# Full 128-row matmuls in the attention of a two-layer streaming encoder

## The chip, the core and the metric

The kernel runs as one program on one core of a Trainium2 chip. The metric is the device time of one execution in microseconds. Every kernel is run several times, and the median is given. The trace of one execution was taken by the hardware profiler.

## What is computed

One inference step of a hybrid encoder trunk with two layers, for 512 new frames of one stream (the prompt) and 32 frames of a running stream (the sample, with 128 cached positions). Per layer:

```python
h = rmsnorm(x)
cq, ckv, kr, hq, hf, hi, hg, ga, gb = split(h @ w_in)        # one input projection
q = rmsnorm(cq) @ w_uq          # 8 heads, 128 plain + 64 rotary columns each
k_nope, v = rmsnorm(ckv) @ w_ukv ; k_pe = rope(kr)           # k_pe is shared by the heads
o_a = softmax((q_nope k_nope^T + rope(q_pe) k_pe^T) / sqrt(192)) v   # block-causal for the prompt
o_b = gated linear recurrence (4 heads)                      # causal, chunk by chunk
x = x + (sigmoid(ga) * (o_a @ w_a) + sigmoid(gb) * (o_b @ w_b)) @ w_out
x = x + conv_ffn(rmsnorm(x))                                 # 1024 -> 2 x 2816 -> 1024
```

All inputs and outputs are float32. The sample's 32 queries see all 160 of their own keys (128 cached, 32 new), without a mask.

## The kernel before, in words

Activations lie with features on the 128 partitions and 544 tokens (512 + 32) along the free dimension. Each float32 operand of a product is split into a high and a low part of a reduced float32 type (`split`, lines 152 to 154: ScalarE makes the high part, VectorE subtracts it), and a product is three matmuls: high by high, low by high, high by low. The large products are made by `linear` (line 185); its matmuls have line 198.

Smaller work (the recurrence of a head, the attention of a head) is written as generators that a queue called `side` steps through between the matmuls of the large products, at a pace that is set by hand: ten steps of one head's attention are spread over the products that stand beside it (lines 860 to 871). The program is laid down in that order, a planner at compile time then fixes each engine's stream, and it may move an instruction within its engine's stream. Each engine runs its stream in order and waits on semaphores of the others.

The attention of a head is `attend` (line 725). `rope_q` leaves the rotary queries of a head as four stacked groups of 32 rows: high, high, low, low. The rotary keys' high part `krh` holds the 64 key rows twice, on 128 rows, so that one matmul with `krh` (line 737) gives high and low query by high key. Their low part `krl` is kept on 64 rows only, and is multiplied with the first 64 rows of the queries (line 738). A block of scores (`scores`, line 734) is thus five matmuls into one PSUM bank, the last of them over 64 rows. There are four prompt blocks of 128 queries in a head (256, 256, 384 and 512 keys wide), tile `sc`, and one sample block of 160 keys, tile `ss`.

A prompt block goes on to `softmax` (line 717: maximum, scaled negation, exponential with sum on ScalarE, reciprocal, multiplication), to `turn` (transposes of 128 x 128, line 764), and to `weigh` (line 778). The sample block is computed for 128 queries, of which the last 32 rows are copied out of PSUM by ScalarE (line 793) and go through softmax as a tile `sP` of 32 rows. `sample_turn` transposes it in two pieces (lines 799 and 800: 32 rows by 128 and 32 rows by 32), splits each piece, and `sample_weigh` multiplies by the values in six matmuls (line 812): three over 128 rows, three over 32 rows.

PSUM tiles of the small work come from a ring of four banks (`s_ps`). Weights are cast by ScalarE; the subtraction for some of them runs on GpSimd (`pool=True`, line 176).

Of the kernel before, what the change touches and what calls it, by code (L numbers as in the profile page):

```python
# [18 lines left out]
P = 128  # L19
L = 2  # L20
# [31 lines left out]
class Late:  # L52
    """A value whose instructions come with its first use, or within the product before."""

# [9 lines left out]
class Pieces:  # L64
    """Weights of n row blocks, of which each group of eight is fetched at its first use."""

# [12 lines left out]
class Side:  # L79
    """Work whose instructions are laid between those of the large products."""  # L80

# [7 lines left out]
    def pace(self, rate):  # L89
        """Steps to take for each tick of the large products."""  # L90
        self.rate, self.owed = rate, 0.0
# [23 lines left out]
def trunk(ctx, tc, io):  # L115
# [123 lines left out]
    class Norm:  # L239
        """Sum of squares over feature blocks, as they come."""  # L240

# [15 lines left out]
    def prep(x, gcol, norm, name, vector=False):  # L257
        """Split of gain * x, and its share of the norm's sum."""
        if norm is not None:
            norm.add(x, vector)  # L260
        hi, lo = bt(f"hhi_{name}"), bt(f"hlo_{name}")
        g = vec[:, gcol:gcol + 1]
        nc.scalar.activation(hi, x, AF.Copy, scale=g)
        nc.vector.scalar_tensor_tensor(lo, x, g, hi, op0=ALU.mult, op1=ALU.subtract)
        return hi, lo
# [29 lines left out]

    # Lower bounds of the forget gates: softmax over the layers, cumulated.
    lbs, omls = [], []
# [33 lines left out]
    for l in range(L):  # L331
# [21 lines left out]
        if l == 0:  # L353
            # The first products run while the norm is still on its way.
            early[U_HF] = product(U_HF, "hf0_", first)
            early[U_HQ] = product(U_HQ, "hq0_")
            ws = load_w(io["w_in"][l, U_HI], ND, P, "hi0_0")
            r.get()
            early[U_HI] = linear(ws, h, TH, "ps_hi0_0", apart=True)
# [5 lines left out]
        with ExitStack() as mixer:  # L365
# [3 lines left out]
            krh = mp.tile([P, KW], F32R, name=f"krh{l}")  # L369
            krl = mp.tile([64, KW], F32R, name=f"krl{l}")  # L370
            gates = dram.tile([2 * ND, P, T], F32, name=f"gates{l}")
            ob = []

            with ExitStack() as hs:
# [17 lines left out]
                def levels(q0, Q, K, F1, FL, A, ntok, top, name):  # L392
                    """Decayed products q k within chunks of 128 rows, by halves of ever larger
                    blocks: every factor is a product of forget gates, at most one."""
                    nch = ntok // P
# [36 lines left out]
                def scan(hh, q0, Q, K, f, vt):  # L432
                    """Outputs and final state of a head over the prompt."""
                    nm = f"{l}_{hh}"
# [38 lines left out]
                def scan_sample():  # L473
                    """The four heads' sample rows as one block of 128."""
                    flat = lambda x: x.rearrange("p h t -> p (h t)")
# [79 lines left out]

                # Compressed queries, latents, rotary keys, merge gates.
                def gate(i):
# [32 lines left out]
                def rotary_keys(z):  # L590
                    zsw = tt(f"zks{l}")
                    for q in range(4):
                        src, dst = z[(q ^ 1) * 32:(q ^ 1) * 32 + 32, :], zsw[q * 32:q * 32 + 32, :]
                        nc.scalar.activation(dst, src, AF.Copy, scale=-1.0 if q % 2 == 0 else 1.0)
                    kr = h1.tile([P, KW], F32, name=f"kr{l}")
                    nc.sync.dma_start(kr[0:64, SP:SP + PAST], io["c_kr"][l])
                    nc.sync.dma_start(kr[64:128, SP:SP + PAST], io["c_kr"][l])
                    nc.vector.tensor_mul(z, z, cos)
                    nc.vector.tensor_mul(zsw, zsw, sin)
                    nc.vector.tensor_add(kr[:, 0:SP], z[:, 0:SP], zsw[:, 0:SP])  # L600
                    nc.vector.tensor_add(kr[:, SP + PAST:KW], z[:, SP:T], zsw[:, SP:T])
                    nc.sync.dma_start(io["krope"][l, :, 0:SP], kr[0:64, 0:SP])
                    nc.sync.dma_start(io["krope"][l, :, SP:T], kr[0:64, SP + PAST:KW])
                    nc.scalar.copy(krh, kr)
                    nc.vector.tensor_sub(krl, kr[0:64, :], krh[0:64, :])

# [23 lines left out]
            def merge(j):  # L630
                """A block of both branches' gated sum."""
                sg, mb = tt(f"sga{l}_{j}"), tt(f"mb{l}_{j}")
# [10 lines left out]

            # Attention.
            oa = []
            with ExitStack() as asx:
# [10 lines left out]
                def rope_q(hq):  # L657
                    """Rotated queries of four heads, as rows (high, high, low, low)."""
                    raw = fetch_w(io["w_qr"][l, hq], 2 * QR_K * P, f"qr{l}_{hq}")
# [25 lines left out]
                def project(hd):  # L685
                    """Queries, keys and (for two heads) values of a head."""
                    nm = f"{l}_{hd}"
# [37 lines left out]
                def attend(hd):  # L725
# [8 lines left out]
                    def scores(ps, qs, ks):  # L734
                        for i, (a, b) in enumerate(rows):
                            nc.tensor.matmul(ps, a[:, qs], b[:, ks], start=(i == 0), stop=False)  # L736
                        nc.tensor.matmul(ps, q4[:, qs], krh[:, ks], start=False, stop=False)
                        nc.tensor.matmul(ps, q4[0:64, qs], krl[:, ks], start=False, stop=True)

# [11 lines left out]
                    def turn(half, pr, kps):  # L751
                        """Probabilities with the keys on partitions, split."""
                        nkb = 2 * half + 2
# [31 lines left out]

                    # The sample's rows are the last 32 of the last 128 queries.
                    NK = PAST + SS

                    def sample_scores():
                        ps = s_ps(f"ss{nm}")  # L790
                        scores(ps[:, :NK], slice(T - P, T), slice(SP, KW))
                        sP = ap.tile([SS, NK], F32, tag="sP", name=f"sP{nm}")
                        nc.scalar.copy(sP, ps[P - SS:P, :NK])
                        softmax(sP, sP, SS, f"{nm}_s")
                        return sP

                    def sample_turn(sP):
                        ps = s_ps(f"spt{nm}")
                        nc.tensor.transpose(ps[:, 0:SS], sP[:, 0:PAST], ident[0:SS, 0:SS])
                        nc.tensor.transpose(ps[0:SS, SS:2 * SS], sP[:, PAST:NK], ident[0:SS, 0:SS])  # L800
                        sph = ap.tile([P, 2 * SS], F32R, tag="sph", name=f"sph{nm}")
                        spl = ap.tile([P, 2 * SS], F32R, tag="spl", name=f"spl{nm}")
                        split(sph[:, 0:SS], spl[:, 0:SS], ps[:, 0:SS])
                        split(sph[0:SS, SS:2 * SS], spl[0:SS, SS:2 * SS], ps[0:SS, SS:2 * SS])
                        return sph, spl

                    def sample_weigh(sph, spl):
                        ps = s_ps(f"spo{nm}")
                        i = 0
                        for a, rr in ((0, P), (1, SS)):  # L810
                            for v, p in ((vh, sph), (vl, sph), (vh, spl)):
                                nc.tensor.matmul(
                                    ps[:, 0:SS], v[0:rr, 4 + a, vo:vo + P], p[0:rr, a * SS:(a + 1) * SS],
                                    start=(i == 0), stop=(i == 5),
# [28 lines left out]
                def gated_b(j):  # L843
                    """The gated share of branch b."""
                    if not ob:
# [42 lines left out]

        # Gated feed-forward network.
        with ExitStack() as fs:  # L890
# [13 lines left out]
            def final(t, ps, x):  # L904
                """Half of the tokens' output, when their last block is there."""
                hs = slice(t * TH, (t + 1) * TH)
# [9 lines left out]
                for j in range(0, ND, 2):  # L916
                    # The first half's share stays in place, the second's goes out in pairs of blocks.
                    pair = bt(f"yo{j}", F32) if t else None
# [44 lines left out]
            def down(j):  # L963
                """The weights of an output block; the last has its own place for most of them."""
                return Pieces(lambda k: load_w(
# [42 lines left out]
def _units(w, cols):  # L1008
    """Columns of [L, K, N] weights as [L, unit, 128 rows, K/128 x unit width]."""
    l, k, _ = w.shape  # L1010
# [5 lines left out]
def _rows(v):  # L1016
    """[..., n * 128] vectors as [128, ... x n]."""
    return np.ascontiguousarray(np.asarray(v).reshape(-1, P).T)
# [81 lines left out]
```

## Time and profile before

| | |
|---|---|
| median of 3 runs | 1913.16 us |
| lowest and highest | 1912.61 and 1913.16 us |
| span of the profiled execution, first to last instruction | 1910.8 us |
| between that span and the median of the runs | 2.4 us |
| TensorE busy | 1887.2 us (99% of the span) |
| VectorE, ScalarE, GpSimd busy | 1092.7, 797.1, 312.2 us |

The profiled execution has no time of its own beside its span; the runs' median stands in for it, and the 2.4 us are what lies before the first and after the last instruction. Busy TensorE is not TensorE at its peak: its instructions overlap and their ends are modelled, so what one costs is read from the distance between the starts of one and the next. The attention of the first layer lies at about 271 to 467 us of the span, that of the second at about 1213 to 1409 us.

### The profile page before, as it was taken

How to read it: one execution, taken by the hardware profiler on the slowest of the kernel's cores; microseconds unless marked ns; L12 is line 12 of the kernel's file. 1: busy time of each engine (PE TensorE's matmuls, PEld its weight loads, DVE VectorE, ACT ScalarE, POOL GpSimd, SP SyncE). 2: the span in 40 equal slices, each digit the busy share in tenths (PEclk: the TensorE clock that was granted, in tenths of full speed). 3: DMA queues.
4: the chain of work that ended last, by engine and by line, in shares of the span. 5: the costliest groups of instructions: out<-in, count | busy, mean ns of one | idle time of the engine just before them, and what ended most of it. 6: DMA issues, size and time to landing. Idle time of an engine off the chain costs nothing.

```text
span 1910.8 us, 36056 instructions
## 1 busy us (share of the span) xinstructions
PE 1887.2 (99%) x14680; PEld 1847.6 (97%) x14680; DVE 1092.7 (57%) x2113; ACT 797.1 (42%) x1454; POOL 312.2 (16%) x474
## 2 busy tenths in 40 slices
PE   7999999999999999999999999999999999999997
PEld 7999999899999999999999999998999999999997
DVE  7765865666465555533375667656655655555224
ACT  4222866554344333332232248564533433333231
POOL 3011021221212222100011110212112122222001
PEclk9999999999999999999999999999999999999999
DMA  5121432333542222234322124323235422222332
GB/s 181 57 70 67 131 122 83 95 102 104 194 158 89 89 89 89 89 95 125 102 91 70 57 80 143 119 80 107 93 126 190 138 85 87 87 88 87 103 96 75
DMA packets 75526, 197.29 MB, mean 103 GB/s; under 512 B 10208, under 2 KB 14304, under 8 KB 75360
## 3 DMA queue, kind: packets, MB, share of 16 engines
q1 hardware_dynamic: 75360, 194.98, 30.9%
q8 instruction: 116, 1.90, 0.4%
q14 instruction: 50, 0.41, 0.1%
HBM read 165.68 MB, written 24.81 MB: 100 GB/s over the span
## 4 chain that ended last, share of the span: by engine, by line
PE 97%; DVE 1%; DMA 1%; issue 0%; SPq 0%; ACT 0%; DVEq 0%; ACTq 0%
PE ps_uv L198 14%; PE ps_ua L198 14%; PE ps_d L198 13%; PE ps_gate L198 10%; PE ps_pa L198 5%; PE ps_o L198 5%; PE A L401 3%; PE ps_q L198 3%; PE ps_pb L198 3%; PE ps_hg L198 3%; PE ps_hq L198 2%; PE ps_hi L198 2%; PE ps_hf L198 2%; PE ps_cq L198 2%; PE sc L736 2%; PE ps_v L710 2%
## 5 line engine op out<-in xcount | busy, mean ns | idle before, releaser
L176 DVE TENSOR_TENSOR wlo_d<-raw_d,whi_d 128x512 fp32r<-128x512 f32 x96 | 62.5, 655 | 149.5 <-ACT whi_d L175 149.5
L198 PE MATMUL ps_uv<-hlo_f,whi_uv 128*128 128x272 f32 x704 | 145.9, 289 | 0.0
L198 PE MATMUL ps_ua<-hlo_f,whi_ua 128*128 128x272 f32 x704 | 145.9, 289 | 0.0
L198 PE MATMUL ps_ua<-hhi_f,wlo_ua 128*128 128x272 f32 x704 | 145.8, 288 | 0.0
L198 PE MATMUL ps_ua<-hhi_f,whi_ua 128*128 128x272 f32 x704 | 145.6, 288 | 0.0
L198 PE MATMUL ps_uv<-hhi_f,whi_uv 128*128 128x272 f32 x704 | 145.6, 288 | 0.0
L198 PE MATMUL ps_uv<-hhi_f,wlo_uv 128*128 128x272 f32 x704 | 145.4, 288 | 0.0
L198 PE MATMUL ps_d<-il,whi_d 128*128 128x272 f32 x660 | 136.9, 289 | 0.0
L198 PE MATMUL ps_d<-ih,wlo_d 128*128 128x272 f32 x660 | 136.6, 288 | 0.0
L198 PE MATMUL ps_d<-ih,whi_d 128*128 128x272 f32 x660 | 136.2, 288 | 0.0
L175 ACT CAST whi_d<-raw_d 128x512 fp32r<-128x512 f32 x96 | 55.8, 585 | 175.5 <-PE ps_d L198 143.7
L175 ACT CAST whi_ua<-raw_ua 128x512 fp32r<-128x512 f32 x88 | 54.7, 621 | 165.3 <-PE ps_ua L198 157.9
L175 ACT CAST whi_uv<-raw_uv 128x512 fp32r<-128x512 f32 x96 | 59.6, 621 | 142.5 <-PE ps_uv L198 134.1
L198 PEld LDWEIGHTS ps_ua<-hhi_f,wlo_ua 128*128 128x128 f32 x704 | 110.8, 188 | 0.2
L198 PEld LDWEIGHTS ps_ua<-hhi_f,whi_ua 128*128 128x128 f32 x704 | 110.9, 188 | 0.0
L198 PEld LDWEIGHTS ps_uv<-hhi_f,whi_uv 128*128 128x128 f32 x704 | 110.9, 188 | 0.0
L198 PEld LDWEIGHTS ps_uv<-hhi_f,wlo_uv 128*128 128x128 f32 x704 | 110.7, 188 | 0.0
L198 PEld LDWEIGHTS ps_ua<-hlo_f,whi_ua 128*128 128x128 f32 x704 | 110.4, 188 | 0.0
L198 PEld LDWEIGHTS ps_uv<-hlo_f,whi_uv 128*128 128x128 f32 x704 | 110.4, 188 | 0.0
L198 PEld LDWEIGHTS ps_d<-ih,whi_d 128*128 128x128 f32 x660 | 103.6, 188 | 0.0
L198 PEld LDWEIGHTS ps_d<-il,whi_d 128*128 128x128 f32 x660 | 103.6, 188 | 0.0
L198 PEld LDWEIGHTS ps_d<-ih,wlo_d 128*128 128x128 f32 x660 | 103.2, 188 | 0.0
(469 smaller groups left out, 5274.8 us busy)
## 6 DMA issues: line engine op xcount, KB each, us to landing
raw_ua<-in_w_up SPq DMA_DIRECT2D x44, 512.0 KB, 3.2
raw_uv<-in_w_up SPq DMA_DIRECT2D x44, 512.0 KB, 3.2
raw_gate<-in_w_in SPq DMA_DIRECT2D x32, 512.0 KB, 3.7
raw_d<-in_w_dn SPq DMA_DIRECT2D x32, 512.0 KB, 3.5
gates<-z_gate SPq DMA_DIRECT2D x32, 272.0 KB, 2.9
raw_pa<-in_w_pa SPq DMA_DIRECT2D x16, 512.0 KB, 3.5
raw_wo<-in_w_o SPq DMA_DIRECT2D x16, 512.0 KB, 3.7
raw_d<-in_w_dn SPq DMA_DIRECT2D x16, 384.0 KB, 3.1
```

Of the source, the lines that this page charges most:

```text
L175: nc.scalar.copy(hi[:, :n], part)
L176: (nc.gpsimd if pool else nc.vector).tensor_sub(lo[:, :n], part, hi[:, :n])
L198: nc.tensor.matmul(ps[t][:, 0:n], w, x[:, t * n:(t + 1) * n], start=(i == 0), stop=(i == last),)
L401: nc.tensor.matmul(ps[:, s], kk[:, s], qq[:, s], start=True, stop=True)
L710: nc.tensor.matmul(ps[:, :2 * P], lat[k][x][:, s], wv[k][w], start=(i == 0), stop=(i == 5))
L736: nc.tensor.matmul(ps, a[:, qs], b[:, ks], start=(i == 0), stop=False)
```

## The change

The low part of the rotary keys is kept on all 128 rows, so that the matmul of line 738 runs over 128 rows. (Its two further groups of rows add low query by low key, a term that was left out before.) The sample's softmax runs on all 128 query rows, straight out of PSUM, into a tile of the ring that the prompt blocks use (`tag="p"`, four buffers); the columns 160 to 255 of that tile are zeroed by GpSimd. The transposes become two of 128 x 128, the split takes the last 32 columns of both in one ScalarE and one VectorE instruction, and the sample's six weighting matmuls all run over 128 rows (the padded rows are zero). The diff also removes comments and docstrings; its core:

```diff
-            krl = mp.tile([64, KW], F32R, name=f"krl{l}")
+            krl = mp.tile([P, KW], F32R, name=f"krl{l}")
...
-                    nc.vector.tensor_sub(krl, kr[0:64, :], krh[0:64, :])
+                    nc.vector.tensor_sub(krl, kr, krh)
...
-                        nc.tensor.matmul(ps, q4[0:64, qs], krl[:, ks], start=False, stop=True)
+                        nc.tensor.matmul(ps, q4[:, qs], krl[:, ks], start=False, stop=True)
...
-                        sP = ap.tile([SS, NK], F32, tag="sP", name=f"sP{nm}")
-                        nc.scalar.copy(sP, ps[P - SS:P, :NK])
-                        softmax(sP, sP, SS, f"{nm}_s")
+                        sP = ap.tile([P, 512], F32, tag="p", name=f"sP{nm}", bufs=4)
+                        nc.gpsimd.memset(sP[:, NK:2 * P], 0.0)
+                        softmax(sP[:, :NK], ps[:, :NK], P, f"{nm}_s")
                         return sP
 
                     def sample_turn(sP):
                         ps = s_ps(f"spt{nm}")
-                        nc.tensor.transpose(ps[:, 0:SS], sP[:, 0:PAST], ident[0:SS, 0:SS])
-                        nc.tensor.transpose(ps[0:SS, SS:2 * SS], sP[:, PAST:NK], ident[0:SS, 0:SS])
-                        sph = ap.tile([P, 2 * SS], F32R, tag="sph", name=f"sph{nm}")
-                        spl = ap.tile([P, 2 * SS], F32R, tag="spl", name=f"spl{nm}")
-                        split(sph[:, 0:SS], spl[:, 0:SS], ps[:, 0:SS])
-                        split(sph[0:SS, SS:2 * SS], spl[0:SS, SS:2 * SS], ps[0:SS, SS:2 * SS])
+                        pw = ps[:, 0:2 * P].rearrange("p (a q) -> p a q", a=2)
+                        for a in range(2):
+                            nc.tensor.transpose(pw[:, a, :], sP[:, a * P:(a + 1) * P], ident)
+                        sph = ap.tile([P, 2, SS], F32R, tag="sph", name=f"sph{nm}")
+                        spl = ap.tile([P, 2, SS], F32R, tag="spl", name=f"spl{nm}")
+                        split(sph, spl, pw[:, :, P - SS:P])
                         return sph, spl
...
-                        for a, rr in ((0, P), (1, SS)):
+                        for a in range(2):
                             for v, p in ((vh, sph), (vl, sph), (vh, spl)):
                                 nc.tensor.matmul(
-                                    ps[:, 0:SS], v[0:rr, 4 + a, vo:vo + P], p[0:rr, a * SS:(a + 1) * SS],
+                                    ps[:, 0:SS], v[:, 4 + a, vo:vo + P], p[:, a, :],
```

## Rows read from the trace of the kernel before

**Rows 1.** The cores: span and mean granted TensorE clock.

```profile
core 0: 1910.8 us, clock 0.997
```

**Rows 2.** The chain that ended last: shares of the span by engine.

```profile
PE 97%; DVE 1%; DMA 1%; issue 0%; SPq 0%; ACT 0%; DVEq 0%; ACTq 0%
```

**Rows 3.** First layer's attention, engines' busy us (instructions) in the columns' order.

```profile
core 0: us, PE busy (x) PEld busy (x) DVE busy (x) ACT busy (x) POOL busy (x), PEclk, DMA share, GB/s
271.20:466.70 195.50, 194.59 (x1372) 177.17 (x1370) 123.39 (x356) 102.90 (x269) 31.66 (x32) 1.00 0.31 98
```

**Rows 4.** Line 738's matmuls: ns min/median/max, first and last start, shapes.

```profile
L738 PE MATMUL sc<-krl,qr x64: 379/408/498, 294.0 to 1398.4; 64*128 64x256 f32 x32, 64*128 64x384 f32 x16, 64*128 64x512 f32 x16
...
L738 PE MATMUL ss<-krl,qr x16: 337/338/342, 303.8 to 1400.2; 64*128 64x160 f32 x16
```

**Rows 5.** Timeline of PE, first and second score block of a head: start, length.

```profile
342.65 0.28 PE L737 MATMUL sc<-krh,qr 128*128 128x256 f32 x1
342.86 0.38 PE L738 MATMUL sc<-krl,qr 64*128 64x256 f32 x1
343.17 0.39 PE L736 MATMUL sc<-kh,qh 128*128 128x256 f32 x1
343.40 0.28 PE L736 MATMUL sc<-kh,ql 128*128 128x256 f32 x1
343.52 0.28 PE L736 MATMUL sc<-kl,qh 128*128 128x256 f32 x1
```

**Rows 6.** Timeline of PEld, weight loads around the third score block's end.

```profile
345.62 0.19 PEld L737 LDWEIGHTS sc<-krh,qr 128*128 128x128 f32 x1
346.06 0.18 PEld L738 LDWEIGHTS sc<-krl,qr 64*128 64x128 f32 x1 [0.25 <-issue]
```

**Rows 7.** Timeline of PE around a sample score block's end.

```profile
372.77 0.28 PE L737 MATMUL ss<-krh,qr 128*128 128x160 f32 x1
...
373.61 0.41 PE L198 MATMUL ps_q<-cqh,whi_qk 128*128 128x272 f32 x2
373.86 0.42 PE L198 MATMUL ps_q<-cqh,wlo_qk 128*128 128x272 f32 x2
```

**Rows 8.** Timeline of PE: three full transposes, then the sample's two.

```profile
335.74 0.49 PE L764 MATMUL pt<-ident,p 128*128 128x128 f32 x3
335.99 0.50 PE L198 MATMUL ps_gate<-hlo_in,whi_gate 128*128 128x272 f32 x2
336.32 0.41 PE L198 MATMUL ps_gate<-hhi_in,whi_gate 128*128 128x272 f32 x2
...
337.08 0.41 PE L198 MATMUL ps_gate<-hhi_in,whi_gate 128*128 128x272 f32 x2
...
337.98 0.41 PE L198 MATMUL ps_gate<-hlo_in,whi_gate 128*128 128x272 f32 x2
```

**Rows 9.** Timeline of PE, the sample's weighting of the same head.

```profile
340.45 0.26 PE L812 MATMUL spo<-sph,vl 128*128 128x32 f32 x1
340.56 0.26 PE L812 MATMUL spo<-spl,vh 128*128 128x32 f32 x1
...
341.19 0.52 PE L198 MATMUL ps_pb<-obh,whi_pb 128*128 128x272 f32 x2
341.54 0.29 PE L198 MATMUL ps_pb<-obh,wlo_pb 128*128 128x272 f32 x1
```

**Rows 10.** Timeline of DVE, softmax of the first blocks; idle before, releaser.

```profile
346.58 0.11 DVE L744 MEMSET sc<- 64x64 f32 x1 [1.51 <-PE sc L738]
...
347.46 0.53 DVE L723 TENSOR_SCALAR p<-p,st 128x128 f32<-128x128 f32 x2
```

**Rows 11.** Timeline of PE, the first transpose that reads those probabilities.

```profile
348.04 0.27 PE L764 MATMUL pt<-ident,p 128*128 128x128 f32 x1
```

**Rows 12.** POOL's waits in the first layer's attention: us, times, longest.

```profile
POOL wlo_qk L176 <- ACT whi_qk L175: 57.7, 15, 14.9
```

**Rows 13.** POOL's costliest groups: busy us, mean ns of one, idle before.

```profile
L582 POOL MEMSET lr<- 128x96 f32 x4 | 0.7, 178 | 45.0 <-DVE latl L154 45.0
```

## Prediction

> **What bounds the kernel now.** I read the cores first: one core, 1910.8 us from first to last instruction, clock 0.997, so TensorE runs at its upper level of 2.4 GHz nearly throughout and the clock has nothing to give [rows 1]. Then the chain that ended last: 97% of it is TensorE [rows 2]. A change that takes time out of TensorE's stream therefore shortens the whole, as far as nothing else comes to stand in its place. Third, the table by stretch for the attention of the first layer, the stage that the change touches: TensorE is busy 194.6 of 195.5 us there, VectorE 123.4, ScalarE 102.9, GpSimd 31.7 [rows 3]. Only a shorter TensorE stream can help in this stage, and the other three have room. The second layer's attention is the same program on other weights, and the score matmuls start in both, from 294 to 1398 us [rows 4].
>
> "Busy" hides how well TensorE is used, so the fourth view is the timeline, where I compare starts. In a run of full matmuls 256 columns wide the next one starts 0.12 us after the last (343.40 to 343.52). Around the 64-row matmul it is otherwise: it starts 0.21 us after the full one ahead of it, the next full one 0.31 us after it, and the one behind that another 0.23 us later [rows 5]. The weight loads tell why. The load for the full matmul at line 737 starts ahead of its matmul, while another one streams; the 64-row load starts after 0.25 us in which no load was under way [rows 6], at the very start of its own matmul. Going from 128 rows to fewer, and back, TensorE empties before it goes on.
>
> **The change part by part.**
>
> *Line 738.* From line 737's start to the second full matmul behind the 64-row one, 342.65 to 343.40, is 0.75 us for three steps; three full steps would be 3 x 0.12 = 0.36. One visit to 64 rows costs 0.39 us [rows 5]. The sample's blocks of 160 columns: from 372.77 to 373.61 lie two score matmuls and a pair of a large product, 0.84 us; a pair alone is 0.25 (373.61 to 373.86) [rows 7], and a full step with few columns is 0.11 (340.45 to 340.56, bound by its weight load) [rows 9], so 0.84 - 0.25 - 2 x 0.11 = 0.37. There are 64 prompt and 16 sample blocks [rows 4]. I price the 384 and 512 columns as the 256, because what is lost is the emptying, not the streaming. 64 x 0.39 + 16 x 0.37 = 30.9 us. The matmul over 128 rows is taken at a full step; its like, line 737 with the same queries and columns, is one of the rows [rows 5].
>
> *Sample transposes.* Two large-product pairs with the sample's two transposes between them start 0.90 us apart (337.08 to 337.98); without the pairs' 2 x 0.25, the two transposes cost 0.40. Three full transposes take 0.25 (335.74 to 335.99) and the pair behind them 0.33 instead of 0.25 [rows 8], so two full ones cost 2 x 0.083 + 0.08 = 0.25. Gain 0.15, sixteen times 2.4 us. The bounds are nothing (two full ones as dear as the mixed ones) and 0.24 each, if the 0.08 behind them is not theirs: 0 to 3.8 us.
>
> *Sample weighting.* From the second of the six matmuls to the second pair behind them is 1.09 us (340.45 to 341.54) [rows 9]. With full rows it is five steps of 0.11 and a pair of 0.25, 0.80. Gain 0.29, sixteen times 4.6 us. The rows of the padding cost no step of their own.
>
> Together 30.9 + 2.4 + 4.6 = 37.9 us off TensorE's stream, about 19 in each layer's attention.
>
> *Beside the path.* The low part of the keys is subtracted once a layer on twice the rows, in the same column count. ScalarE loses a copy and a cast for each head, VectorE a subtraction; the sample's reduction, exponential and multiplication keep their 160 columns. I price these at nothing: VectorE is free for 72 and ScalarE for 93 of 195.5 us, and even with 19 us gone they are at 70% and 58% [rows 3]; uncovered they would be well under 1 us a head. New is GpSimd's zeroing of 96 columns; the same shape took 0.18 us elsewhere [rows 13], 2.9 us in all on an engine with 16% load, and it needs only an earlier block's buffer. The PSUM bank of the sample's scores is held through the maximum and the exponential now instead of one copy; it goes into the bound below.
>
> *What is late next.* The transposes of a head wait for probabilities. VectorE ends the first two blocks' probabilities at 347.99 (347.46 + 0.53) [rows 10], and the first transpose that needs both starts at 348.04 [rows 11]: 0.05 us to spare. In each layer six such half-turns start within 0.25 us of their probabilities. The chain ahead of them is tied to TensorE: VectorE idles 1.51 us for a score block's last matmul [rows 10], so most of it comes earlier by the same amount as TensorE. What does not is the way out of the last block: from the end of its 64-row matmul (start + 0.38) to the second full start behind it (+ 0.54) there is 0.16 us, against about 0.24 - 0.28 = -0.04 with a full one [rows 5]. TensorE thus gains 0.20 us on each such chain: 12 x 0.20 = 2.4 us given back as waits. Three value weightings a layer have as little to spare behind their values' casts; I put one block's 0.39 on each as an estimate, 6 x 0.39 = 2.3. Together 5 us. The bounds: nothing, if the slack suffices, and the exit plus a whole further block, 0.30 + 0.39 = 0.69 us, at each of the 32 half-turns, 22 us, if the chains do not follow at all.
>
> The sum: 37.9 - 5 = 33 us. Against the profiled execution, 1910.8 + 2.4 - 33 = 1880; the 2.4 us are what the median of the runs, 1913.16, has over the span.
>
> **A rule against it.** The rows show full loads laid under the matmul ahead and the 64-row load not [rows 6]. The Trainium skill, "TensorE: Matmul & The Clock Gate", Part 3, "The mechanism", says under "What overlaps and what doesn't" that a weight load overlaps matmuls in flight only where its row group is another one. By that, padding to all four groups would leave every such load exposed, and the time would stay at 1913; by the rows it is 1880. The trace disagrees with the rule here, and a further sentence of the same page (Part 2, "Step-by-step", loads into a background buffer) leaves room for what the rows show.
>
> **The rivals.**
>
> *No give-back, 1875.* The planner or the slack covers all waits: 1913.2 - 37.9. For it: 19 us more in each layer's attention leave VectorE at 70% at most [rows 3]. Against it: the 0.05 us to spare [rows 10, 11].
>
> *The chains take half, 1891 to 1897.* The softmax chains and the PSUM ring become the bound: 22 us of waits, 1913.2 - 37.9 + 22 = 1897, less if only some do. For it: the ring of four banks, one of them held longer. Against it: VectorE waits for TensorE, not the other way round [rows 10].
>
> *The change does nothing, 1913.* The long steps belong to this load of these queries, not to the number of rows; then a full matmul there steps as badly. For it stands only the page's rule above; against it, line 737 loads the same queries on 128 rows and is hidden [rows 6].
>
> *Slower, through GpSimd.* Its stream is in order, and it waits up to 14.9 us (15 waits, 57.7 us) for a weight cast before a subtraction [rows 12]. If the planner puts the zeroing behind such a subtraction, the sample's second transpose waits for it, and TensorE with it. The mean of the waits, 57.7 / 15 = 3.8 us, at each of the 16 heads is 61 us: 1875 + 61 = 1936. It decides from 37.9 / 16 = 2.4 us a head on. Against it: the zeroing needs only a buffer that was free some steps before the sample's scores, so its place is most likely ahead.
>
> **How the numbers follow.** Forecast with small waits, 1876 to 1887: 0.53. No give-back: 0.17. The chains take half: 0.20. Nothing: 0.05. Slower: 0.05. The predicted time is the likeliest, 1880. The range goes from 1873, which is the full gain with the transposes at their upper bound (1.4 us more) and rounding, to 1897, the upper bound of the waits; nothing and slower, 0.10, are left out with some tails. A measurement here can tell about 0.2%, 3.8 us, from no change. Faster by more: 0.53 + 0.17 + 0.20 = 0.90; within: 0.05; slower: 0.05.
>
> **What would show it.** Right: no 64- or 32-row form left on TensorE, a step of about 0.12 us on both sides of line 738, the attention of a layer near 179 us instead of 195.5, and all else of the same length. The give-back would show as TensorE waiting for VectorE's probabilities or parts at the transposes and weightings, some 2.5 us a layer. Wrong: steps of line 738 that stay at 0.21 and 0.31 us; waits of over 5 us a layer; or TensorE waiting for GpSimd ahead of the sample's second transpose.

## The result, and the profile after

| | before | changed |
|---|---|---|
| median, us | 1912.88 | 1881.72 |
| runs | 4, 1912.30 to 1913.16 | 4, 1881.31 to 1882.74 |
| span of the profiled execution, us | 1910.8 | 1879.5 |

The ratio is 0.9838, with a 95% interval of 0.9824 to 0.9852: 31.2 us less, where 1880 and 33 less were predicted. The span has lost 31.3 us.

The page of the changed kernel: span, TensorE's busy time, and the shares of the chain that ended last.

```profile
span 1879.5 us, 36066 instructions
PE 1852.8 (99%) x14680; PEld 1840.8 (98%) x14680; DVE 1094.0 (58%) x2097; ACT 787.8 (42%) x1422; POOL 314.6 (17%) x490
PE 96%; DVE 3%; issue 1%; DMA 1%; ACT 0%; DVEq 0%; SPq 0%; ACTq 0%
```

TensorE carries out 14680 matmuls, as many as before, and is 99% "busy", as before. The share does not tell the two kernels apart; the distances between the matmuls' starts do. The chain answers to [rows 2]: VectorE, 1% there, has 3% here.

The first layer's attention, by stretch (columns as in [rows 3]), and the pieces of the chain that begin where this attention and that of the second layer end:

```profile
271.20:451.18 179.98, 177.87 (x1371) 174.04 (x1371) 123.95 (x348) 98.13 (x253) 32.83 (x40) 1.00 0.34 107
```

```profile
451.18 43.06 PE ps_pa L198 x342
...
1377.46 43.02 PE ps_pa L198 x342
```

The stretch takes 180.0 us instead of 195.5 [rows 3], 15.5 less. In the second layer the chain puts it at 1213.47 to 1408.75 us before and at 1197.73 to 1377.46 after, 195.3 and 179.7 us, 15.6 less. Together that is 31.1 of the 31.3 us. Nothing outside attention moved by an amount that matters.

Line 738's matmuls now have 128 rows:

```profile
L738 PE MATMUL sc<-krl,qr x64: 277/310/397, 293.9 to 1368.0; 128*128 128x256 f32 x32, 128*128 128x384 f32 x16, 128*128 128x512 f32 x16
L738 PE MATMUL ss<-krl,qr x16: 273/275/278, 302.1 to 1369.4; 128*128 128x160 f32 x16
```

TensorE's timeline shows places like those of [rows 5, 7, 8, 9]: two score blocks, a sample block (of another head than in [rows 7]), the sample's transposes, its weighting.

```profile
338.08 0.28 PE L737 MATMUL sc<-krh,qr 128*128 128x256 f32 x1
338.20 0.28 PE L738 MATMUL sc<-krl,qr 128*128 128x256 f32 x1
338.32 0.28 PE L736 MATMUL sc<-kh,qh 128*128 128x256 f32 x1
338.44 0.27 PE L736 MATMUL sc<-kh,ql 128*128 128x256 f32 x1
...
345.63 0.27 PE L737 MATMUL ss<-krh,qr 128*128 128x160 f32 x1
...
346.14 0.47 PE L198 MATMUL ps_k<-lath,whi_qk 128*128 128x336 f32 x2
...
332.90 0.41 PE L198 MATMUL ps_gate<-hhi_in,whi_gate 128*128 128x272 f32 x2
333.15 0.38 PE L801 MATMUL spt<-ident,sP 128*128 128x128 f32 x2
333.29 0.49 PE L198 MATMUL ps_gate<-hhi_in,wlo_gate 128*128 128x272 f32 x2
333.62 0.41 PE L198 MATMUL ps_gate<-hlo_in,whi_gate 128*128 128x272 f32 x2
...
336.08 0.26 PE L812 MATMUL spo<-sph,vl 128*128 128x32 f32 x1
...
336.64 0.50 PE L198 MATMUL ps_pb<-obh,whi_pb 128*128 128x272 f32 x2
336.97 0.41 PE L198 MATMUL ps_pb<-obh,wlo_pb 128*128 128x272 f32 x2
```

Every step around line 738 is 0.12 us, and the 0.75 us of [rows 5] have become 0.36: 0.39 less, as priced. The sample block and the pair behind it take 0.51 us (345.63 to 346.14), 0.33 less than the 0.84 of [rows 7]. The two transposes stand between pairs that start 0.72 us apart, 0.18 less than the 0.90 of [rows 8]. The weighting takes 0.89 us (336.08 to 336.97), 0.20 less than the 1.09 of [rows 9].

TensorE's weight loads show what they waited for in the whole execution (us, times, longest):

```profile
PEld pt L764 <- DVE p L723: 3.9, 6, 1.2
PEld ps_pb L198 <- DVE ql L154: 1.6, 4, 0.6
PEld pt L764 <- DVE ptl L154: 1.1, 2, 0.6
```

In the kernel before, the same view has the third and the first of these with other sums, and the second not at all:

```profile
PEld pt L764 <- DVE ptl L154: 1.8, 2, 0.9
...
PEld pt L764 <- DVE p L723: 0.4, 2, 0.2
```

The balance of these is 3.9 - 0.4 + 1.6 + 1.1 - 1.8 = 4.4 us more of waits for VectorE. Other waits in attention fell by 0.8 us (0.5 for a weight cast of ScalarE, 0.3 ahead of the sample's transposes), which leaves 3.6. Without them the gain would have been larger, and why they came where they did is the second question for the experiments.

### The profile page after: what moved, and what is told of

It is laid out like the page before. It is cut to its first block, busy times and chain, and to the rows that moved or that the text cites. A ratio compares the mean times of both kernels' runs of the same rounds, so it can differ in the third digit from the quotient of the medians.

```text
span 1879.5 us, 36066 instructions
## 1 busy us (share of the span) xinstructions
PE 1852.8 (99%) x14680; PEld 1840.8 (98%) x14680; DVE 1094.0 (58%) x2097; ACT 787.8 (42%) x1422; POOL 314.6 (17%) x490
## 4 chain that ended last, share of the span: by engine, by line
PE 96%; DVE 3%; issue 1%; DMA 1%; ACT 0%; DVEq 0%; SPq 0%; ACTq 0%
PE ps_uv L198 14%; PE ps_ua L198 14%; PE ps_d L198 13%; PE ps_gate L198 10%; PE ps_pa L198 5%; PE ps_o L198 5%; PE A L401 3%; PE ps_hg L198 3%; PE ps_pb L198 3%; PE ps_hq L198 2%; PE ps_hi L198 2%; PE ps_hf L198 2%; PE ps_q L198 2%; PE ps_cq L198 2%; PE ps_v L710 2%; PE po L778 2%
```

## The experiments

Two questions: what exactly does TensorE pay for, a change of the row count (theory A) or each matmul on fewer rows (rival B); and where do the waits that came back come from? All times are medians; ratios are to the kernel before, run beside it.

### Each part alone

Keys alone, on the kernel before:

```diff
-                        nc.tensor.matmul(ps, q4[0:64, qs], krl[:, ks], start=False, stop=True)
+                        nc.tensor.matmul(ps, q4[:, qs], krl[:, ks], start=False, stop=True)
```

(with `krl` made on 128 rows). The other run has all of the change but this.

> The kernel before, with the low part of the rotary keys on all 128 rows and nothing else changed. Theory A (TensorE empties at each change of the row count, and pays per visit to fewer rows): 64 visits of 0.39 us and 16 of 0.33 us go, 30.2 us; some 3 us come back as waits of the transposes for VectorE. About 1886 us. Rival A2 (the waits that came back belong to the sample's new softmax, its zeroing or its longer hold of the PSUM bank): no waits here, 1883 us or less. Rival B (the gain came mostly from the sample's part): above 1900 us.

> The kernel before, with the sample's softmax, transposes and weighting on 128 rows, and line 738 still on 64 rows. Theory A: 16 heads x (0.18 us at the transposes + 0.20 us at the weighting) = 6.1 us, about 1907 us, with next to no new waits, because TensorE is hardly faster. Rival A2 (the sample's part brings the waits of the changed kernel, 3 us or more): 1910 us or above.

Keys alone: 1887.93 us, ratio 0.9869 (0.9854 to 0.9883), 25.3 us less. Sample alone: 1907.07 us, 0.9967 (0.9955 to 0.9980), 6.1 us less, as expected. The parts add up: 25.3 + 6.1 = 31.4. The keys fall 2 us short of what theory A gave them. Their waits:

```profile
PEld pt L764 <- DVE p L723: 3.2, 6, 0.9
PEld pt L764 <- DVE ptl L154: 1.8, 2, 0.9
```

The waits for probabilities are there without any of the sample's change, so A2 is out: it is the faster TensorE that meets VectorE, not the zeroing by GpSimd or the PSUM bank that is held longer. In the run with the sample's part alone, the two waits sum to 2.3 us, about the 2.2 of the kernel before.

### Per change or per matmul

Three runs move 32- and 64-row matmuls about in the kernel before, with the same computation. The first alternates the row counts in the sample's weighting:

```diff
-                        for a, rr in ((0, P), (1, SS)):
-                            for v, p in ((vh, sph), (vl, sph), (vh, spl)):
+                        for v, p in ((vh, sph), (vl, sph), (vh, spl)):
+                            for a, rr in ((0, P), (1, SS)):
```

> The kernel before; the sample's six weighting matmuls come in the order 128, 32, 128, 32, 128, 32 rows instead of three and three. The work is the same. Theory A (the price is per change of row count): three visits to 32 rows for one, two more at 0.20 to 0.33 us in 16 heads, 6 to 11 us slower, 1919 to 1924 us. Rival B (each matmul on fewer rows has its price, whatever stands beside it): no change, 1913 us.

1919.81 us, ratio 1.0035 (1.0022 to 1.0048): 6.6 us slower, by nothing but the order. Its timeline (a row holds one matmul over 128 rows and one over 32):

```profile
340.76 0.39 PE L812 MATMUL spo<-sph,vh 128*128 128x32 f32 x2
341.08 0.49 PE L812 MATMUL spo<-sph,vl 128*128 128x32 f32 x2
341.50 0.49 PE L812 MATMUL spo<-spl,vh 128*128 128x32 f32 x2
341.92 0.52 PE L198 MATMUL ps_pb<-obh,whi_pb 128*128 128x272 f32 x2
```

A round of one full and one 32-row matmul takes 0.42 us (341.08 to 341.50), where two full ones take 0.22 (two steps of 0.11 [rows 9]): 0.20 for each visit, and two visits more in 16 heads are 6.4 us.

The second puts two 64-row matmuls of different blocks side by side (`low=False` leaves the fifth matmul out of `scores`, and `block` goes on with the bank that it is given):

```diff
+                    def first_two():
+                        both = [s_ps(f"sc{nm}_{qb}") for qb in range(2)]
+                        for qb in range(2):
+                            scores(both[qb][:, :2 * P], slice(qb * P, (qb + 1) * P), slice(0, 2 * P), low=False)
+                        for qb in range(2):
+                            nc.tensor.matmul(both[qb][:, :2 * P], q4[0:64, qb * P:(qb + 1) * P], krl[:, 0:2 * P], start=False, stop=True)
+                        return [block(qb, both[qb]) for qb in range(2)]
...
-                    p01 = [block(0), block(1)]
+                    p01 = first_two()
```

> The kernel before; in the first two score blocks of a head the two 64-row matmuls stand side by side, behind the eight full ones, instead of one behind each block. The work is the same. Theory A: 16 visits fewer, 16 x 0.39 = 6.2 us off, about 1907 us, up to 1 us less gain because the first block's softmax starts later. Rival B (a price per matmul on fewer rows): no change, 1913 us.

1906.66 us, ratio 0.9964 (0.9951 to 0.9977): 6.5 us less, with not one matmul fewer. The timeline:

```profile
342.08 0.28 PE L737 MATMUL sc<-krh,qr 128*128 128x256 f32 x1
342.29 0.50 PE L746 MATMUL sc<-krl,qr 64*128 64x256 f32 x2
342.72 0.52 PE L198 MATMUL ps_pb<-obh,wlo_pb 128*128 128x272 f32 x2
343.08 0.41 PE L198 MATMUL ps_pb<-obl,whi_pb 128*128 128x272 f32 x2
```

The way in is again 0.21 us and the way out 0.36 for a pair, but once for two: 1.00 us from 342.08 to 343.08, against 3 x 0.12 + 0.25 = 0.61 with full rows. The visit costs 0.39 us whether one matmul or two are in it.

The third makes two 64-row matmuls of half the columns out of each one:

```diff
-                        nc.tensor.matmul(ps, q4[0:64, qs], krl[:, ks], start=False, stop=True)
+                        m = (ks.stop - ks.start) // 2
+                        for c in range(2):
+                            kc = slice(ks.start + c * m, ks.start + (c + 1) * m)
+                            nc.tensor.matmul(ps[:, c * m:(c + 1) * m], q4[0:64, qs], krl[:, kc], start=False, stop=(c == 1))
```

> The kernel before; the 64-row matmul of line 738 is made as two 64-row matmuls of half the columns each, side by side. Theory A: still one visit for each block, and only the steps of more and narrower matmuls are added, at most 0.11 us a block (bound by the weight load), 0 to 9 us, 1913 to 1922 us. Rival B (a price of 0.33 to 0.39 us for each matmul on fewer rows): 80 x 0.37 = 30 us slower, 1943 us.

1914.00 us, ratio 1.0007 (0.9998 to 1.0017): 1.2 us more, with no difference inside the interval, at the low end of theory A and 29 us from rival B. The three together settle it: the price is for going to fewer rows and back.

### Where the gain that came back was lost

The longest wait of TensorE in attention, 1.2 us, and the others for `p` end with multiplications of line 723 on VectorE. In the changed kernel one of them runs like this, with GpSimd's timeline under it:

```profile
359.28 0.28 DVE L723 TENSOR_SCALAR p<-p,st 128x128 f32<-128x128 f32 x1
...
359.67 1.46 DVE L723 TENSOR_SCALAR p<-p,st 128x256 f32<-128x256 f32 x1
```

```profile
359.69 1.29 POOL L176 TENSOR_TENSOR wlo_uv<-raw_uv,whi_uv 128x512 fp32r<-128x512 f32 x1 [5.71 <-ACT whi_uv L175]
```

The multiplication of 128x256 takes 1.46 us, and lies over a subtraction of GpSimd from start to end. Of line 723's 80 multiplications in this trace (64 for the prompt, 16 for the sample) 12 take over 0.6 us; each of the 12 overlaps a subtraction of GpSimd and ends 0.10 to 0.33 us after it, and none without such an overlap takes over 0.49 us. Theory C says that the one holds up the other.

The one shown ends at 361.13, and with it a wait of 0.6 us. The longest, 1.2 us by the weight loads and 0.90 in the matmul's own row, ends otherwise (TensorE's timeline, then VectorE's):

```profile
369.85 0.55 PE L764 MATMUL pt<-ident,p 128*128 128x128 f32 x3 [0.90 <-DVE p L723]
```

```profile
369.31 0.49 DVE L723 TENSOR_SCALAR p<-p,st 128x512 f32<-128x512 f32 x1
```

This multiplication has its normal length, and is only late. VectorE is busy 14.4 of the 15 us from 358 to 373, and 2.8 of the 4.0 us of the first layer's waits end between 361 and 373.3. A multiplication held up at 363.80, 1.62 us long, stands in its queue 5.5 us earlier; that its delay is what is carried on to 369.31 is likely, but not shown.

The first run takes the multiplication off VectorE:

```diff
-                    nc.vector.tensor_scalar_mul(out, out, st[:n, 2:3])
+                    nc.scalar.activation(out, out, AF.Copy, scale=st[:n, 2:3])
```

> The changed kernel, with the last step of the softmax (probabilities times the reciprocal of their sum) on ScalarE instead of VectorE. Theory C (the waits that came back stem from VectorE's multiplications, some of which take 1.3 to 1.6 us instead of 0.4 while GpSimd subtracts): the long ones go, TensorE's waits for them go from 3.9 us to under 1, 1878 to 1880 us. Rival D (the waits are the length of the softmax chain, whichever engine it is on): 1881 to 1885 us, ScalarE named as the releaser.

1880.99 us, ratio 0.9833 (0.9816 to 0.9849). The waits for VectorE's `p` are gone as C had it, but the time is the changed kernel's within the scatter, and C's 1878 to 1880 are missed. Other waits came in their place, mostly for VectorE (weight loads of the whole execution, as above):

```profile
PEld ps_pb L198 <- DVE ql L154: 2.7, 6, 0.8
PEld ps_gate L198 <- DVE ql L154: 1.4, 2, 0.7
PEld pt L764 <- ACT p L723: 0.9, 4, 0.3
```

D's releaser, ScalarE, is there with 0.9 us. This run does not decide between the two.

The second takes GpSimd away instead, in the four weight loads beside attention (`w_qr`, `w_qk`, `w_uv`, `w_pb`; one of them here):

```diff
-                    ws = load_w(io["w_qk"][l, hd], QR_K + KV_K, P, f"qk{nm}", pool=True)
+                    ws = load_w(io["w_qk"][l, hd], QR_K + KV_K, P, f"qk{nm}")
```

> The changed kernel, with the subtractions of the attention's weights on VectorE instead of GpSimd. Theory C (VectorE's multiplications are held up by GpSimd's subtractions): no multiplication takes over 0.6 us, but VectorE takes 32 subtractions of 0.65 us a layer more; the waits at 360 and 369 us of the span fall, others may come; 1878 to 1883 us. Rival D (the length of the multiplications has nothing to do with GpSimd): they keep their 1.3 to 1.6 us, and the time rises with VectorE's load, 1883 to 1890 us.

1878.69 us, ratio 0.9823 (0.9808 to 0.9838), 3 us under the changed kernel. The multiplication shown above, at the same place of the same head in this run:

```profile
361.66 0.35 DVE L723 TENSOR_SCALAR p<-p,st 128x256 f32<-128x256 f32 x1
```

The kernel was run again below. The first two of the next fences are line 723's multiplications (ns min/median/max) in the changed kernel and in that second run, the third is TensorE's waits there:

```profile
L723 DVE TENSOR_SCALAR p<-p,st x64: 252/409/1623, 297.7 to 1371.3; 128x128 f32<-128x128 f32 x16, 128x256 f32<-128x256 f32 x16, 128x384 f32<-128x384 f32 x16, 128x512 f32<-128x512 f32 x16
```

```profile
L723 DVE TENSOR_SCALAR p<-p,st x64: 243/380/489, 297.2 to 1368.4; 128x128 f32<-128x128 f32 x16, 128x256 f32<-128x256 f32 x16, 128x384 f32<-128x384 f32 x16, 128x512 f32<-128x512 f32 x16
```

```profile
PEld ps_q L198 <- DVE zgb L853: 2.1, 2, 1.0
PEld pt L764 <- DVE p L723: 1.3, 4, 0.5
```

None takes over 0.49 us now, where the longest took 1.62, and TensorE's waits for them are 1.3 us instead of 3.9. VectorE got the subtractions in exchange, and a new wait of 2.1 us with them. Rival D is out as to the length of the multiplications. How much of the 3 us is due to the multiplications alone is not separated: this edit takes every overlap with GpSimd's weight subtractions away, and the run before it, which took the multiplications off VectorE, gained nothing clear.

The third moves VectorE's rotary work to another head:

```diff
-                    if hd == 4:
+                    if hd == 3:
                         rope_q(1)
```

(and the extra ticks of that head with it).

> The changed kernel, with the rotary queries of heads 4 to 7 made one head earlier, beside a head without value products. Theory E (the longest wait, 1.1 us a layer at a transpose, comes from VectorE's rotary work standing in the queue ahead of the probabilities in the same head as the value products): the waits fall by 1 to 1.5 us a layer, 1878 to 1880 us. Rival D: the wait moves along with the rotary work, 1881 to 1883 us.

1880.85 us, ratio 0.9833 (0.9818 to 0.9848): rival D but for 0.15 us; the waits for `p` fall to 1.6 us, and others come at the value products, as the weight loads' waits show:

```profile
PEld ps_v L710 <- ACT p L721: 2.2, 4, 1.1
PEld ps_v L710 <- DVE vl L154: 1.6, 2, 0.8
```

Last, the changed kernel, the run without GpSimd's weight subtractions, and the latter with each of the two other edits, side by side.

> The changed kernel itself once more, beside the next three, so that they can be compared on the same chip: 1881 to 1883 us.

> The changed kernel with the attention's weight subtractions on VectorE, once more: theory C, 2 to 4 us below the changed kernel, about 1879 us; if the first result was scatter, no difference.

> The changed kernel with the weight subtractions on VectorE and the last step of the softmax on ScalarE. If VectorE's queue is what still holds TensorE up, both together give 1877 to 1879 us, with under 1 us of TensorE's waits left in each layer's attention; if the length of the chain is, ScalarE's slower multiplication makes it 1879 to 1882 us.

> The changed kernel with the weight subtractions on VectorE and the rotary queries of heads 4 to 7 made a head earlier. If the load of VectorE beside the value products is what is left, 1877 to 1879 us; if the wait only moves along, 1879 to 1882 us.

| run | edits on the changed kernel | median, us | ratio to before |
|---|---|---|---|
| changed | none | 1881.54 | 0.9838 (0.9824 to 0.9851) |
| no GpSimd, again | `pool=True` removed | 1878.53 | 0.9819 (0.9806 to 0.9833) |
| and ScalarE multiplies | the edit of line 723 too | 1878.92 | 0.9821 (0.9808 to 0.9834) |
| and rotary early | `hd == 3` too | 1880.97 | 0.9832 (0.9818 to 0.9845) |

The gain of 3.0 us repeats: the runs lie from 1878.41 to 1878.85 and from 1881.13 to 1883.93 us, without overlap. It is 0.16%, and the intervals of the ratios overlap, so it is small, but it came both times. Neither of the two other edits adds to it: with ScalarE's multiplication the time is 0.4 us longer, within 1877 to 1879, but some 3 us of waits are left in each layer where under 1 was expected. The early rotary work takes 2.4 of the 3.0 us away again, as its second case (the wait only moves along) had it. The version without GpSimd's weight subtractions is the fastest that was run.

## Why the prediction was right

*What bounds the kernel.* TensorE's stream set the time, and the time that left it left the whole: 31.3 us of span, 31.1 of them from the two stretches of attention.

*Line 738.* Right, and to the hundredth in the prompt blocks, the wider ones too: 64 x 0.39 = 25.0 us. In the sample blocks the term was 0.04 us too large, since the pair behind a full block of 160 columns takes 0.29 us and not 0.25. 16 x 0.33 = 5.3.

*Sample transposes and weighting.* The first was worth 0.18 us instead of 0.15, the second 0.20 instead of 0.29. The working of the weighting put a pair of 0.25 us behind six narrow full matmuls; it is 0.33 (336.64 to 336.97). Together 16 x 0.38 = 6.1 us instead of 7.0, and the run of the sample's part alone has measured just that. The whole gain on TensorE's stream was thus 25.0 + 5.3 + 6.1 = 36.4 us and not 37.9, from one place of each kind; read over all blocks and heads of both traces it is 36.0.

*The reason.* That a change of the row count costs TensorE time was read from a few places in the trace; the three runs that only move matmuls show that the price is per visit: +6.6 us for 32 more visits, -6.5 us for 16 fewer, no clear difference for twice the matmuls in as many visits. The Trainium skill has it so in "TensorEngine Tiling (Array Packing)", "Key Properties": a change of tiling mode drains TensorE, with no figure. The trace agrees in that each change is paid for, and gives 0.39 us for a visit to 64 rows between matmuls of 256 columns, 0.20 for one to 32 rows between narrow ones; that TensorE stands empty in between is not seen by itself, since the ends of matmuls are modelled.

*The rule weighed against it.* The exposed loads were those of 64 rows, and with them went their idle time. In the kernel before, the list of what the weight loads waited for begins with a row that names no other engine ("issue"):

```profile
PEld sc L738 <- issue: 9.6, 32, 0.4
```

and the same list of the changed kernel has no row for line 738. As the prediction read it, what the Trainium skill, "TensorE: Matmul & The Clock Gate", Part 3, "The mechanism", says of loads and row groups would have left the time at 1913. The runs differ: the loads of 128 rows among 128 rows are the hidden ones.

*What came back.* Of the size 5 us were predicted, and 36.4 - 31.3 = 5.1 came, or 4.7 by the reading over all heads. The reason was only partly right, so it is partly luck that the sizes meet. Predicted was a short wait of 0.20 us on each of twelve chains and of 0.39 at six weightings; instead a few long ones came, 3.9 us in six waits for probabilities and 1.6 in four for the queries' low part, and no weighting waited.

The half-turn that was given 0.05 us to spare [rows 10, 11] runs on without a wait among these. It had more. The transpose of [rows 11] is the first of three, and reads the first block's probabilities only. TensorE's weight loads of the kernel before show that it did not wait for 347.99:

```profile
347.92 0.14 PEld L764 LDWEIGHTS pt<-ident,p 128*128 128x128 f32 x1
...
348.18 0.25 PEld L764 LDWEIGHTS pt<-ident,p 128*128 128x128 f32 x2
```

The first that needs the second block is loaded at 348.18, with 0.19 us to spare.

The prediction priced VectorE by its share of the whole stretch, 72 of 195.5 us free. Most of the waits came where VectorE is nearly full, 14.4 of 15 us. Part of their length, shown by the run without GpSimd's weight subtractions, is a multiplication that lasts 1.5 us beside GpSimd's subtraction and 0.35 us without it. The prediction did not look at what overlaps VectorE's work, though the trace of the kernel before has such a multiplication too, of 1.50 us:

```profile
L723 DVE TENSOR_SCALAR p<-p,st x64: 217/409/1496, 298.1 to 1401.5; 128x128 f32<-128x128 f32 x16, 128x256 f32<-128x256 f32 x16, 128x384 f32<-128x384 f32 x16, 128x512 f32<-128x512 f32 x16
```

Of what came back, 3.6 us are the balance of attention's waits; the rest, 1.1 to 1.5 us, is not placed.

*The rivals.* No give-back (1875) missed by 6.7 us, and the chains that take half (1891 to 1897) by 9 or more. The zeroing by GpSimd, the slower case, showed nowhere: no wait of TensorE names GpSimd's zeroing, and the sample's part alone brings its full gain.

## What to carry to other kernels

Read the distance between starts on both sides of every matmul with another row count; a row or two of the timeline shows a price that "99% busy" hides. If rows can be padded with zeros or with terms that belong to the sum, a full matmul among full ones can cost less than a smaller one, as it did here; if not, put the small ones side by side, which here gave back 6.5 us by order alone. And when the bound engine is made faster in a stretch (here by 8%), look there for the few microseconds in which the next engine has no idle time, and for its longest single instructions: the average share of 63% [rows 3] hid both here.

## What the runs showed of the hardware that was not expected

A VectorE multiplication of float32 by a column (128x256) took 1.46 us while GpSimd subtracted for 1.29 us, and 0.35 us, at the same place of the same head, in the run without GpSimd's weight subtractions. The longest of the 64 fell from 1.62 to 0.49 us there. The Trainium skill, "SBUF — State Buffer", "Who interferes with whom", says that VectorE, in some forms and modes that such a multiplication can enter, shares a pair of ports with GpSimd, and that whichever issues first keeps it for its whole instruction while the other is blocked. The trace agrees that one instruction was held for the other's whole length; the multiplication's recorded start is 0.02 us ahead of GpSimd's, so who issued first is not shown for this pair. In another of the changed kernel GpSimd starts 0.10 us ahead, and the sample's multiplication, whose median is 0.30 us, ends 0.10 us after it:

```profile
370.53 1.29 DVE L723 TENSOR_SCALAR sP<-sP,st_s 128x160 f32<-128x160 f32 x1
```

```profile
370.43 1.29 POOL L176 TENSOR_TENSOR wlo_qk<-raw_qk,whi_qk 128x512 fp32r<-128x512 f32 x1 [5.24 <-PE pt L764]
```
